# A diffusion trunk on one core: exchange loads on SyncE's queue, odd normalisation steps in x's tiles, first combinations ahead of the second split

## The chip, the core and the metric

The kernel runs on one core of a Trainium2 chip. TensorE (PE) multiplies, VectorE (DVE), ScalarE (ACT) and GpSimd (POOL) work on the elements, SyncE (SP) issues transfers, and ACT can issue them too, on a queue of its own. Each engine works through its own list in order; semaphores make one wait for another. The metric is the device time of one execution in microseconds: the median of three runs.

## The reference

One layer of a backbone with a context prefix, in float32: x is 2048 x 1024, the context 256 x 1024.

```
h  = rmsnorm(x) * (1 + sc1) + sh1
p  = h @ w_in                              # 1024 x 3584
o  = concat(hgrn2(p), gmlp_gate(p))        # two gated scans; gelu(u) * (W_s LN(gelu(v)) + b)
x  = x + g1 * (o @ w_out)                  # 1024 x 1024
h2 = rmsnorm(x) * (1 + sc2) + sh2
a, g = split(h2 @ w_up)                    # 1024 x 5632
m  = a * gelu(conv3x3(g) + conv_b)
x  = x + g2 * (m @ w_down)                 # 2816 x 1024
out = rmsnorm(x)
```

## The kernel before

**Arithmetic.** Each float32 operand is split into a rounded high part and the rest, both `fp32r`: a cast on ACT (`S.copy`, line 140) makes the high part, a subtraction (line 141) on DVE or POOL the low one. A product of two split operands is three matmuls (hi·hi, hi·lo, lo·hi). The projections behind the scans also use Strassen's scheme in Winograd's form: of four quarter blocks of each operand seven combinations are made, and seven products take the place of eight.

**Stages.** After the input projection, the scans and the gate (to about 925 us) comes the output projection: eight units of 256 rows, seven products each, 56 in all, numbered m here. Each product is 12 matmuls of 128x512 (`products`, line 1304): for k = 0 to 3 hi·hi and hi·lo in turn, then the four lo·hi. So the low part of the right operand B[i] is needed from the second matmul on, and its second half (k = 2, 3) from the sixth. Then the FFN's up-projection runs over the two halves of the tokens: 22 units each (`g` feeds the convolution, `a` is multiplied by its GELU), 154 products per half, numbered n. Here the right operands B[0] to B[6] are the seven combinations of the normalised y of one half; they stay for a whole half and are exchanged at n of about 143 to 166. The down-projection follows.

**Left operands.** `Unit.prep(i)` (line 1248) makes the split `Ah`, `Al` of combination i of a unit, three products ahead (`LOOK`): a cast on ACT, a subtraction on GpSimd. It also makes the next combinations in place: a21 = a11 - a21 (line 1264), s2 = a22 - a21 (1266), a11 = s2 + a11 (1268), a12 = a12 - s2 (1270), on DVE for the output projection and for the units marked `light`, on GpSimd otherwise. The first unit's halves lie in `ahead[0]` and `ahead[1]` (tiles `first`), its s2 in `ahead[4]`, the first two split pairs in `pairs_a`. `LEAD` interleaves the first two units: (0,0), (0,1), (0,2), (1,0), (0,4), (1,1), (0,3) and so on. Products 0 and 2 of a unit add into the same bank `ux`, which line 1407 reads and adds to the row tile after each product.

**Right operands.** B[i][1] is loaded raw; `in_place(i)` (line 924) casts it to B[i][0] on ACT (one instruction, line 927, always pinned) and subtracts in two halves on DVE (line 930). `apart(i, m)` puts the cast behind product m and the two halves behind product m+1. In the output projection B[1] is split during the last layer norm of the gate (line 716), B[2] beside the mixing that follows it (line 724).

**Normalisations.** `second_norm` (line 1317) works on one unit's rows behind its last product: the scaling (1326), then four steps k, each with four transposes into a bank `dn`, two ACT instructions (1341) into a tile of seven combinations, three DVE subtractions (1344 to 1346) and a store to `yd` (1347). A step's tile is `yf` for odd k of units 1 to 5, and otherwise `fl`, of which there are two buffers (`c_tile`). `fl` also holds s2 of every second FFN unit. `first` and `step` tell, in microseconds of a planner that counts TensorE's work, when the first step and the next ones may be put in; what is left at the end of the last unit is put in there (line 1431). `v_tile` has three buffers (`cv`): they hold rows of x and later the values of the convolution.

**The convolution's end and the exchange.** A value tile is written by GELU (line 1492), multiplied in place by the `a` products (1564, 1567) and stored by `put_m` (1530 and 1531). Near the end of half 0 the last GELU needs the buffer of the third last one. The raw B[j] of half 1 is issued on ACT's queue (line 1642) one product behind B[j]'s last use in half 0.

**Order.** A list planner orders each engine's instructions by its own estimates. `pin` puts an instruction behind the one traced before it on its engine; instructions without it can move ahead. SP issues the loads and stores in the order so planned and stands at each whose data or buffer isn't ready.

Of the kernel before, what the change touches and what calls it, by code (L numbers as in the profile page):

```python
# [9 lines left out]
F32 = mybir.dt.float32  # L10
# [8 lines left out]
P = 128  # L19
# [70 lines left out]
def tile_trunk(ctx, tc, x, c, cx, c_ctx, w_ada, b_ada, norm_mix, norm_ffn, w_in, hg_norm, sgu_g, sgu_b,  # L90
# [107 lines left out]
    with es1:  # L198
# [480 lines left out]
        def sgu(hh, h):  # L679

            z, u = {}, {}

            def both(n0):
                if n0 in z and n0 in u:
                    zt = z.pop(n0)
                    last = (hh, h) == (1, NH - 1)
                    (V if last else G).tensor_mul(zt, zt, u.pop(n0))
                    (S.dma_start if last and n0 else st)(oT_d[hh][:, 4 + h, n0:n0 + 512], zt)

            def su(n0, n, pj):  # L690
                u[n0] = pm.tile([P, 512], F32, tag="gu", name="gu", bufs=2)
                S.activation(u[n0], pj, AF.Gelu)
                both(n0)

            def sv(n0, n, pj):
                gv = pm.tile([P, 512], F32, tag="vv", name="gv", bufs=2)
                S.activation(gv, pj, AF.Gelu)

                def ln():
                    pt = bank("mi")  # L700
                    for i in range(4):
                        T.transpose(pt[:, i * P:(i + 1) * P], gv[:, i * P:(i + 1) * P], ident)
                    bs = pm.tile([P, 4, 6], F32, tag="bs", name="bs", bufs=2)
                    mv = pm.tile([P, 4, 2], F32, tag="mv", name="mv", bufs=2)
                    for i in range(4):
                        V.bn_stats(out=bs[:, i, :], in_=pt[:, i * P:(i + 1) * P])
                        V.bn_aggr(out=mv[:, i, :], in_=bs[:, i, :])
                    r = rstd(pm, mv[:, :, 1], 4, 1.0)
                    end = (hh, h) == (1, NH - 1)
                    nt = pm.tile([P, 512], F32, tag="nt", name="nt", bufs=2)  # L710
                    for i in range(4):
                        rooted.append(V.tensor_scalar(
                            out=nt[:, i * P:(i + 1) * P], in0=pt[:, i * P:(i + 1) * P], scalar1=mv[:, i, 0:1],
                            scalar2=r[:, i:i + 1], op0=ALU.subtract, op1=ALU.mult))
                    if end and n0:
                        in_place(1, pin)

                    def mix():
                        pz = bank("mi")
                        for i in range(4):  # L720
                            T.matmul(pz[:, i * P:(i + 1) * P], nt[:, i * P:(i + 1) * P], wsT[:, h, :],
                                     start=True, stop=True)
                        if end:
                            in_place(2, high=n0 == 0, low=n0 == 512)
                        V.scalar_tensor_tensor(out=nt.rearrange("p (c q) -> p c q", q=P),
                                               in0=pz.rearrange("p (c q) -> p c q", q=P), scalar=sgg[:, h:h + 1],
                                               in1=view(rh, h * P, [[0, 4], [1, P]]), op0=ALU.mult, op1=ALU.add)
                        z[n0] = nt
                        both(n0)
                    hg_q.later(mix, 7.0)  # L730
                hg_q.later(ln, 4.6)
            return su, sv

# [488 lines left out]
    def c_tile():  # L1222
        return px.tile([P, NK, P], F32R, tag="fl", name="fl", bufs=2)
# [4 lines left out]

    class Unit:
        def __init__(self, hh, kind, p, slots):  # L1230
            self.slots, self.light = slots, False
            self.hh, self.kind, self.f = hh, kind, 2 * p
            self.raw, self.A, self.s2, self.ready = [], {}, None, {}

# [13 lines left out]
        def prep(self, i):  # L1248

            a11, a21 = self.raw[0][:, :, :P], self.raw[0][:, :, P:]  # L1250
            a12, a22 = (self.raw[1][:, :, :P], self.raw[1][:, :, P:]) if i else (None, None)
            self.A[i] = self.ready.pop(i) if i in self.ready else a_tiles()
            hi, lo = self.A[i]

            if i == 1 and "s2" in self.ready:
                self.s2 = self.ready.pop("s2")
            elif i == 1:
                self.s2 = (c_tile()[:, :4, :].bitcast(F32) if self.slots[0] == 1 and self.kind != "o" else
                           px.tile([P, 4 * P + 80], F32, tag="s1", name="s2")[:, :4 * P].rearrange("p (k c) -> p k c", k=4))
            split(hi, lo, (a11, a12, self.s2, a11, a21, a12, a22)[i])  # L1260
            E = V if self.kind == "o" or self.light else G
            keep = pin if self.light or i == 1 else lambda i: i
            if i == 0:
                keep(E.tensor_sub(a21, a11, a21))
            elif i == 1:
                keep(E.tensor_sub(self.s2, a22, a21))
            elif i == 2:
                keep(E.tensor_add(a11, self.s2, a11))
            elif i == 3:
                keep(E.tensor_sub(a12, a12, self.s2))  # L1270
# [42 lines left out]
    with ExitStack() as esn, ExitStack() as esv:  # L1313
# [3 lines left out]
        def second_norm(n, xs, ss, bank_, first, step):  # L1317

            r = rstd(px, ss, 2, 1.0 / D)
            sc = []  # L1320
            t0 = T.t

            def scale():
                for i in range(2):
                    sc.append((pv[0] if n % 2 and n < NCH - 1 else px).tile([P, D], F32, tag="sc", name="sc", bufs=2))
                    scaled.append(pin(V.tensor_scalar(out=sc[i], in0=xs[i], scalar1=r[:, i:i + 1], scalar2=None,
                                                      op0=ALU.mult)))
            yield scale
            yield max(0.0, t0 + first - T.t)
            cl = slice(n % 4 * P, n % 4 * P + P)  # L1330
            for k in range(4):
                pt = bank_()
                for kk in range(2):
                    for i in range(2):
                        o = kk * 256 + i * P
                        T.transpose(pt[:, o:o + P], sc[i][:, (k + 4 * kk) * P:(k + 4 * kk + 1) * P], ident)
                fl = (pv[0].tile([P, NK, P], F32, tag="yf", name="yf", bufs=2) if k % 2 and 0 < n < NCH - 2 else
                      c_tile().bitcast(F32))
                for kk, dims in ((0, [[7 * P, 2], [1, P]]), (1, [[4 * P, 2], [1, P]])):
                    kq = k + 4 * kk  # L1340
                    pin(S.activation(view(fl, kk * P, dims),
                                     pt[:, kk * 256:kk * 256 + 256].rearrange("p (i c) -> p i c", c=P),
                                     AF.Identity, bias=s2[:, kq:kq + 1], scale=a2[:, kq:kq + 1]))
                pin(V.tensor_sub(fl[:, 3:5, :], view(fl, 7 * P, [[-2 * P, 2], [1, P]]), view(fl, 0, [[7 * P, 2], [1, P]])))
                V.tensor_sub(fl[:, 2, :], fl[:, 5, :], fl[:, 3, :])
                V.tensor_sub(fl[:, 6, :], fl[:, 1, :], fl[:, 2, :])
                st(yd[n // 4][:, :, k, cl], fl[:, :7, :])
                yield step

        pairs = [Unit(n // 4, "o", n % 4, (1, 2) if n % 2 else (3, 0)) for n in range(NCH)]  # L1350
        pairs[0].raw, pairs[0].ready = ahead[:2], {0: ahead[2], 1: ahead[3], "s2": ahead[4]}
        blocks = [(pairs[n], i) for n, i in LEAD] + [(u, i) for u in pairs[2:] for i in SEVEN]

        def prep_o(m):
# [6 lines left out]
            if i == 0 and n > 1:  # L1361
                (pairs + units)[n + 1].load()
            elif n == 1 and i == 2:
                pairs[2].load()
            elif n == NCH - 1 and i in (6, 5):
                units[1].load_half(6 - i)

        xts = {}

# [14 lines left out]
        with tc.issue_after(rooted[-1].ins), tc.issue_after(rooted[-5].ins):  # L1384
            for m in range(LOOK):
                prep_o(m)
        todo = {7: lambda: fetch_x(2, 0), 13: lambda: fetch_x(2, 1)}
        later, scales = {}, {}

        def apart(i, m):  # L1390
# [4 lines left out]
        for m, (u, i) in enumerate(blocks):  # L1395
# [28 lines left out]
                todo[m + 1] = lambda i=i: S.dma_start(B[i][1].bitcast(F32), yd[0][:, i])  # L1424
                apart(i, len(blocks) + (-3, -1, 0, 2, 3, 5, 7)[i])
            if i == 5:
                how = (9.0, 2.8) if n + 1 < NCH else (22.0, 5.5)
                norm = second_norm(n, xs, ss, lambda: dbank()[:, 0, :], *how)
                scales[m + (2 if n + 1 < NCH else 7)] = next(norm)
                if n == NCH - 1:  # L1430
# [186 lines left out]
    for n, (u, i) in enumerate(prods):  # L1617
# [20 lines left out]
            if n in t:  # L1638
                t.pop(n)()
        for j in range(7):  # L1640
            if last_use[j] == n - 1:
                S.dma_start(B[j][1].bitcast(F32), yd[1][:, j])
            elif 7 * NU - 14 + (6, 8, 10, 13, 15, 18, 20)[j] == n:
                apart(j, n)
        prep(n + LOOK)
        for g in later.pop(n, ()):
# [277 lines left out]
```

## Time and profile before

| | before |
|---|---|
| median of three runs | 2393.86 us (2393.09 to 2396.85) |
| the profiled execution | 2402.16 us |
| its span | 2400.4 us |
| mean granted TensorE clock | 0.988 |
| ACT busy | 1057.8 us (44%) |
| GpSimd busy | 945.0 us (39%) |

Lines of the timeline have start, duration, engine, line, operation, tiles and count, and in brackets the idle time in front of it and what ended that. `SPq` and `ACTq` are transfers at their issue; where several are merged, the duration runs from the first issue to the last. Lines of the waits have the engine, line and tile that waited, whom it waited for, total, times and the longest. In the windows, the first number after the stretch is its length, then come the busy times of the engines, the granted clock as a fraction, the mean share of the DMA engines and the rate.

### The profile page before, as it was taken

What the parts mean: (1) busy time and instruction counts of PE and PEld (TensorE: products, weight loads), DVE (VectorE), ACT (ScalarE), POOL (GpSimd) and SP (SyncE); (2) the same over time, 40 slices, a digit from 0 to 9 for tenths busy, and PEclk for the clock granted to TensorE, in tenths of its full rate; (3) what the DMA queues carried; (4) which work ended last, traced back from release to release, by engine and by line L of the source; (5) the groups of instructions that cost most, each with busy time, mean ns of one, the idle gap of its engine ahead of it and who ended that gap; (6) DMA issues with size and microseconds to landing.
All of it is one profiled execution on the core that took longest, in us unless ns stands there. A gap on an engine that the chain in (4) does not pass through costs nothing. (4 is left out here: it accounts for less than half of the span.)

```text
span 2400.4 us, 37036 instructions
## 1 busy us (share of the span) xinstructions
PE 2335.5 (97%) x14059; PEld 1925.5 (80%) x14059; DVE 1694.4 (71%) x2228; ACT 1057.8 (44%) x1811; POOL 945.0 (39%) x817
## 2 busy tenths in 40 slices
PE   7999999999999998998999999899999999999998
PEld 6887878878888876886888888688888888888887
DVE  3757786676686668777986666889677764776876
ACT  3554444443553544545544444354444443332343
POOL 0022111111122234544788787588787860000002
PEclk8999999999999999998999999999999999999999
DMA  8356445664444226766322223522223239834645
GB/s 300 122 187 191 159 145 184 208 228 149 162 159 141 80 93 224 237 229 234 106 82 92 76 91 96 195 75 97 91 84 101 77 126 395 263 123 157 226 148 202
DMA packets 285095, 379.95 MB, mean 158 GB/s; under 512 B 32213, under 2 KB 204525, under 8 KB 282229
## 3 DMA queue, kind: packets, MB, share of 16 engines
q1 hardware_dynamic: 279468, 361.88, 44.9%
q10 hardware_dynamic: 5449, 15.70, 2.0%
q8 instruction: 111, 1.82, 0.3%
q14 instruction: 67, 0.55, 0.1%
HBM read 276.79 MB, written 100.74 MB: 157 GB/s over the span
## 5 line engine op out<-in xcount | busy, mean ns | idle before, releaser
L1482 DVE SCALAR_TENSOR_TENSOR dn<-gp,taps,dn 128x1024 f32<-128x1024 f32 x352 | 450.3, 1286 | 105.5 <-ACT dn L1479 101.0
L141 POOL TENSOR_TENSOR Al<-raw,Ah 128x512 fp32r<-128x512 f32 x306 | 411.9, 1359 | 138.0 <-ACT Ah L140 75.4
L71 PE MATMUL dn<-thl,mhl 128*128 128x512 f32 x1680 | 381.0, 389 | 0.0
L71 PEld LDWEIGHTS dn<-thl,mhl 128*128 128x128 f32 x1680 | 315.3, 188 | 65.5 <-issue 0.2
L71 PE MATMUL pj<-xh,whi 128*128 128x512 f32 x896 | 367.0, 410 | 0.0
L71 PE MATMUL pj<-xl,whi 128*128 128x512 f32 x896 | 351.7, 393 | 0.0
L71 PE MATMUL pj<-xh,wlo 128*128 128x512 f32 x896 | 350.9, 392 | 0.0
L140 ACT CAST Ah<-raw 128x512 fp32r<-128x512 f32 x306 | 189.6, 620 | 256.7 <-PE ux L71 142.9
L71 PE MATMUL ux<-rest,Ah 128*128 128x512 f32 x832 | 208.2, 391 | 0.2
L71 PEld LDWEIGHTS pj<-xh,whi 128*128 128x128 f32 x896 | 168.7, 188 | 38.8 <-issue 7.2
L71 PEld LDWEIGHTS pj<-xh,wlo 128*128 128x128 f32 x896 | 168.5, 188 | 35.7
L71 PEld LDWEIGHTS pj<-xl,whi 128*128 128x128 f32 x896 | 169.0, 189 | 29.1
L71 PE MATMUL uz<-rest,Ah 128*128 128x512 f32 x624 | 186.3, 392 | 1.9 <-DVE rest L930 1.7
L71 PEld LDWEIGHTS ux<-rest,Ah 128*128 128x128 f32 x832 | 155.9, 188 | 33.1 <-issue 0.9
L592 POOL TENSOR_TENSOR K<-K,tot 128x512 f32<-128x512 f32 x40 | 64.2, 1605 | 251.1 <-DVE K L592 139.4
L71 PE MATMUL uz<-four,Ah 128*128 128x512 f32 x412 | 161.1, 391 | 0.5 <-ACT Ah L140 0.5
L141 DVE TENSOR_TENSOR wlo<-raw,whi 128x1024 fp32r<-128x1024 f32 x68 | 83.7, 1231 | 97.6 <-ACT whi L140 95.1
L1780 POOL TENSOR_SCALAR ra<-ss 128x1 f32<-128x1 f32 x8 | 3.9, 490 | 358.9 <-ACT jk L1771 358.9
L71 PEld LDWEIGHTS uz<-rest,Ah 128*128 128x128 f32 x624 | 117.2, 189 | 27.4 <-DVE rest L930 2.5
L140 ACT CAST whi<-raw 128x1024 fp32r<-128x1024 f32 x68 | 71.2, 1048 | 131.9 <-PE pj L71 100.0
L71 PE MATMUL ux<-wo,Ah 128*128 128x512 f32 x408 | 105.4, 400 | 13.4 <-DVE wo L930 7.2
L71 PE MATMUL ux<-four,Ah 128*128 128x512 f32 x416 | 106.5, 397 | 7.2 <-DVE x L1407 3.9
(366 smaller groups left out, 4416.5 us busy)
## 6 DMA issues: line engine op xcount, KB each, us to landing
raw<-in_w_up_dram SPq DMA_DIRECT2D x88, 512.0 KB, 3.6
mr<-m SPq DMA_DIRECT2D x85, 512.0 KB, 6.1
raw<-in_w_in_dram SPq DMA_DIRECT2D x68, 512.0 KB, 4.2
sT<-wd SPq DMA_DIRECT2D x88, 256.0 KB, 5.2
raw<-in_w_ada_dram SPq DMA_DIRECT2D x32, 512.0 KB, 4.0
m<-cv SPq DMA_DIRECT2D x22, 544.0 KB
raw<-in_w_down_dram SPq DMA_DIRECT2D x22, 512.0 KB, 3.7
wd<-raw SPq DMA_DIRECT2D x22, 512.0 KB, 3.7
```

The costliest lines, as they stand in the source:

```text
L71: return self.engine.matmul(out, lhsT, rhs, **kw)
L140: keep(S.copy(hi, raw))
L141: (eng or G).tensor_sub(lo, raw, hi.bitcast(F32))
L592: e.tensor_mul(view(K2, row * W + o, src), view(K, o, src), view(tot, t0, [[4, n], [ts, 2], [0, B]]))
L1482: V.scalar_tensor_tensor(out=cr, in0=gt[:, t // 3:t // 3 + RH, t % 3:t % 3 + GW], scalar=taps[:, t * NF + f:t * NF + f + 1], in1=cr, op0=A ...
L1780: G.tensor_scalar(out=a, in0=ss, scalar1=plus, scalar2=None, op0=ALU.add)
```

## The change

Three edits. **First combinations.** a21 and s2 of the first unit are made on DVE, pinned, in front of the split of B[1] in the gate's last layer norm; B[2]'s low halves and a11 are made behind product 0 of the output projection (`behind_first`), no longer beside the mixing; `prep` leaves out the three combinations so made (`done`); the first two units are `light`, so that their combinations are pinned; the gate's very last multiplication (line 687) moves from DVE to GpSimd, its store stays on ACT's queue. **Normalisation steps.** Steps 1 and 3 of the last unit and step 1 of the last but one take a `v_tile` in place of an `fl` tile; the steps of the last but one are 4.5 planned microseconds apart instead of 2.8. **Exchange.** The loads of B[0] to B[6] for half 1 go to SP's queue, issued three products behind the last use instead of one; the casts of B[1] to B[6] come one to three products later, the low halves with them.

```
-                    (V if last else G).tensor_mul(zt, zt, u.pop(n0))
+                    (V if last and not n0 else G).tensor_mul(zt, zt, u.pop(n0))
...
                     if end and n0:
+                        a, b, s2 = ahead[0], ahead[1], ahead[4]
+                        pin(V.tensor_sub(a[:, :, P:], a[:, :, :P], a[:, :, P:]))
+                        pin(V.tensor_sub(s2, b[:, :, P:], a[:, :, P:]))
                         in_place(1, pin)
...
-                            in_place(2, high=n0 == 0, low=n0 == 512)
+                            n0 or in_place(2, low=False)
...
-            self.slots, self.light = slots, False
+            self.slots, self.light, self.done = slots, False, ()
...
-            if i == 0:
+            if i in self.done:
+                pass
+            elif i == 0:
...
-                fl = (pv[0].tile([P, NK, P], F32, tag="yf", name="yf", bufs=2) if k % 2 and 0 < n < NCH - 2 else
-                      c_tile().bitcast(F32))
+                if k % 2 and 0 < n < NCH - 2:
+                    fl = pv[0].tile([P, NK, P], F32, tag="yf", name="yf", bufs=2)
+                elif n == NCH - 1 and k % 2 or n == NCH - 2 and k == 1:
+                    fl = v_tile()[:, :D].rearrange("p (k c) -> p k c", c=P)
+                else:
+                    fl = c_tile().bitcast(F32)
...
+        pairs[0].done = 0, 1, 2
+        pairs[0].light = pairs[1].light = True
...
+        def behind_first():
+            in_place(2, pin, high=False)
+            a11 = ahead[0][:, :, :P]
+            pin(V.tensor_add(a11, ahead[4], a11))
...
-        todo = {7: lambda: fetch_x(2, 0), 13: lambda: fetch_x(2, 1)}
+        todo = {0: behind_first, 7: lambda: fetch_x(2, 0), 13: lambda: fetch_x(2, 1)}
...
-                how = (9.0, 2.8) if n + 1 < NCH else (22.0, 5.5)
+                how = (9.0, 2.8 if n + 2 < NCH else 4.5) if n + 1 < NCH else (22.0, 5.5)
...
-            if last_use[j] == n - 1:
-                S.dma_start(B[j][1].bitcast(F32), yd[1][:, j])
-            elif 7 * NU - 14 + (6, 8, 10, 13, 15, 18, 20)[j] == n:
+            if last_use[j] == n - 3:
+                ld(B[j][1].bitcast(F32), yd[1][:, j])
+            elif 7 * NU - 14 + (6, 9, 12, 15, 18, 21, 23)[j] == n:
                 apart(j, n)
```

## The prediction

> **What bounds the kernel now.** I read the page's busy shares first, then the list of TensorE's waits over the whole span, then four windows, then the timeline of three of them.
>
> ```profile
> span 2400.4 us, 37036 instructions
> PE 2335.5 (97%) x14059; PEld 1925.5 (80%) x14059; DVE 1694.4 (71%) x2228; ACT 1057.8 (44%) x1811; POOL 945.0 (39%) x817
> ...
> PE ux L71 <- DVE wo L930: 7.2, 1, 7.2
> PE ux L71 <- ACT Ah L140: 6.2, 1, 6.2
> ...
> PE ux L71 <- DVE x L1407: 3.9, 1, 3.9
> ...
> PE ux L71 <- POOL Al L141: 2.9, 1, 2.9
> PE ux L71 <- DVE four L930: 2.4, 2, 2.3
> ```
>
> PE is busy 97% of the span, so only its holes can be won. Of the large single waits (columns: total, times, longest) all but those of the opening ada loads lie on `ux`, in three places, which are the places that the diff touches: the opening of the output projection, its hand-over to the FFN, and the exchange of y's two halves. The windows show what each costs, clock included (columns: length, PE busy, PEld, DVE, ACT, POOL, granted clock, DMA share, GB/s).
>
> ```profile
> 925.91:942.63 16.72, 12.87 (x52) 10.17 (x50) 16.58 (x17) 5.69 (x8) 9.04 (x6) 0.90 0.90 324
> 1102.68:1133.49 30.81, 19.78 (x65) 14.43 (x64) 22.16 (x23) 17.35 (x24) 14.31 (x9) 0.78 0.55 182
> 1536.05:1563.39 27.34, 18.27 (x62) 14.11 (x60) 15.82 (x14) 10.80 (x14) 14.84 (x10) 0.81 0.57 193
> 1170.00:1306.00 136.00, 136.00 (x602) 112.67 (x601) 107.03 (x102) 63.83 (x103) 107.65 (x94) 1.00 0.27 88
> ```
>
> The last row is undisturbed: 136.00/602 = 0.226 us a matmul, 2.71 us for a product of 12. The first window holds 4 products (10.8 us), so it loses 5.9; the second 5 products and four transposes (14.0), so it loses 16.8; the third 5 products (13.6), so it loses 13.8. These 36.5 us are all that this change can win. Part of each loss is the clock, granted at 0.78 to 0.90 there.
>
> **Part A, the opening of the output projection.**
>
> ```profile
> 923.85 2.53 POOL L141 TENSOR_TENSOR pairs_a<-first,pairs_a 128x512 fp32r<-128x512 f32 x2
> ...
> 925.20 3.40 DVE L930 TENSOR_TENSOR wo<-wo,four 128x1024 fp32r<-128x1024 f32 x2
> ...
> 928.52 2.35 DVE L930 TENSOR_TENSOR four<-four 128x1024 fp32r<-128x1024 f32 x2
> ...
> 932.05 0.68 DVE L687 TENSOR_TENSOR nt<-nt,gu 128x512 f32<-128x512 f32 x1
> 932.65 0.68 DVE L1266 TENSOR_TENSOR s<-first,first 128x512 f32<-128x512 f32 x1
> ...
> 933.36 0.62 ACT L140 CAST Ah<-s 128x512 fp32r<-128x512 f32 x1 [6.99 <-DVE s L1266]
> ...
> 935.48 2.83 PE L71 MATMUL ux<-four,Ah 128*128 128x512 f32 x8 [3.85 <-DVE x L1407]
> ...
> 936.95 3.94 DVE L930 TENSOR_TENSOR four<-four,rest 128x1024 fp32r<-128x1024 f32 x2
> ```
>
> DVE is the bound (16.58 of 16.72 busy). ACT waits 6.99 for s2, PE 3.85 for the add of product 0, both queued behind two splits. The change puts the subtractions of L1264 and L1266 (0.68 each) ahead of the first split, the second split's low halves (2.35) behind the add of product 0, and one multiplication of L687 (0.68) on GpSimd, in front of the Al of the next products there; its store stays on ACT's queue. Pinning the first two pairs' combinations adds no instruction.
>
> Worked out: the first DVE split took 3.40 where the second took 2.35, because POOL was busy to 926.4; the two subtractions meet the same 1.05, so they end near 927.7 and the first split near 930.1, 1.5 later than now (928.6). Product 1 starts at 925.91 + 2.71 = 928.6 and needs the second half only at its sixth matmul: it loses 0.5 to 1. L1407 then comes near 931.5, the second split's first half by 932.7 (by 2.35 for two) or 933.5 (by 3.94 for two, contended). So product 2 starts about 2.4 before 935.48, and its eight matmuls (2.83 for 8 x 0.226 = 1.81) win up to 1.0 of clock. Late next is DVE itself: the split of 936.95 must be done before product 4, and has only L687 and one deferred combination less in front, 1.4 us. I take -2.5, nearest to the shift of 2.4; bounds -4 (clock won too) and +1.5 (product 1 delayed, product 4 held by DVE).
>
> **Part B, the last two normalisations.**
>
> ```profile
> 1089.52 0.74 DVE L1326 TENSOR_SCALAR sc<-cv,rs 128x1024 f32<-128x1024 f32 x1
> ...
> 1095.29 0.51 SPq L1347 DMA_DIRECT2D yd<-fl  x1
> ...
> 1104.81 0.56 ACT L1341 ACTIVATE fl<-dn,s,a 128x256 f32<-128x256 f32 x1 [5.46 <-DMA yd<-fl]
> ...
> 1105.86 0.43 DVE L1344 TENSOR_TENSOR fl<-fl 128x256 f32<-128x256 f32 x1 [5.53 <-ACT fl L1341]
> ...
> 1109.01 2.35 DVE L930 TENSOR_TENSOR wo<-wo 128x1024 fp32r<-128x1024 f32 x2
> ...
> 1110.28 2.08 PE L71 MATMUL ux<-wo,Ah 128*128 128x512 f32 x4 [7.21 <-DVE wo L930]
> ...
> 1117.81 0.56 ACT L1341 ACTIVATE fl<-dn,s,a 128x256 f32<-128x256 f32 x1 [4.61 <-PE dn L75]
> ...
> 1119.20 0.68 DVE L1266 TENSOR_TENSOR fl<-raw 128x512 f32<-128x512 f32 x1
> ...
> 1125.45 2.08 PE L71 MATMUL ux<-four,Ah 128*128 128x512 f32 x4 [2.27 <-DVE four L930]
> ```
>
> This is one chain: step 2 of normalisation 6 wants the `fl` buffer of step 0, whose store went out at 1095.29 and released it only at 1104.81; ACT stands 5.46, DVE behind it 5.53, B0's low halves come at 1109.01, PE has stood 7.21. With step 1 in a tile of x's rows, step 2 takes the buffer of normalisation 5's last such step, stored long before; the wait of 5.46 goes. The tile taken is that of row block 6's second half, last read by the scaling at 1089.52. The wider steps (4.5 for 2.8 of the planner's microseconds) put step 1 one product later and step 2 behind the last product, so step 2's ACT and DVE work no longer stands before B0's low halves at all; it stands before B1's, in what is now ACT's idle time of 4.61. Normalisation 7 has no ACT wait on its stores: its tiles are worth nothing by themselves.
>
> B0's low halves come 5.5 earlier (1103.5) and with them PE's restart, 1104.8 for 1110.28. The later splits follow their casts and move along. Four matmuls after the stall took 2.08 for 0.90; with an idle of 1.7 instead of 7.21 some 1.5 of the clock returns. I take -7.0. Bounds: -12 if 2.27 and what follows it go too; 0 if the wait only moves: s2 of the second FFN unit (the L1266 at 1119.20) takes the `fl` buffer that step 2 stores from, and if DVE now reaches it eight microseconds sooner than 1119.20 it can stand there for that store, with B2's split queued behind it.
>
> Of the clock the rows show this: granted 0.78 over the second window, with a wait of 7.21 in it. The Trainium skill, "TensorE: Matmul & The Clock Gate", Part 1, says that the clock halves only after an idle window of about 3.4 us; by that rule the remaining idle of 1.7 would cost no clock, and Part B would give about -8.5, an estimate from that page; the slow matmuls behind the 2.27 at 1125.45 speak against a bound that sharp.
>
> **Part C, the exchange.**
>
> ```profile
> 1532.62 0.33 ACTq L1642 DMA_DIRECT2D four<-yd  x1
> 1534.07 0.34 SPq L1530 DMA_DIRECT2D m<-cv  x1
> ...
> 1543.45 0.97 ACT L1492 ACTIVATE cv<-dn 128x960 f32<-128x960 f32 x1 [11.93 <-DMA as<-cv]
> ...
> 1545.09 3.78 PE L71 MATMUL ux<-wo,Ah 128*128 128x512 f32 x8 [6.16 <-ACT Ah L140]
> ...
> 1558.28 2.08 PE L71 MATMUL ux<-wo,Al 128*128 128x512 f32 x4 [2.90 <-POOL Al L141]
> ...
> 1530.00:1535.00 5.00, 5.00 (x24) 4.14 (x23) 5.00 (x5) 1.52 (x2) 4.65 (x3) 1.00 0.94 321
> 1535.00:1540.00 5.00, 3.93 (x18) 2.92 (x16) 4.71 (x7) 0.00 (x0) 1.25 (x1) 1.00 0.95 297
> ...
> 1551.67 1.91 ACT L927 CAST rest<-rest 128x2048 fp32r<-128x2048 f32 x1
> ...
> 1568.83 1.98 PE L71 MATMUL ux<-four,Ah 128*128 128x512 f32 x8
> ...
> 1570.95 13.52 SPq L1241 DMA_DIRECT2D raw<-in_w_up_dram  x3
> ...
> SPq L1241 <- POOL Al L141: 38.2, 8, 14.5
> ```
>
> ACT's last GELU of half 0 waits for the buffer of an m tile whose store went out at 1534.07 and released it at 1543.45; queued behind it are the Ah of the first product of half 1, which PE waits 6.16 for, and two exchange loads on ACT's queue. Meanwhile the DMA engines are 0.94 to 0.95 busy: B4's 1 MB went out just ahead of that store.
>
> The change issues the loads from SP, two products later, and puts six of the seven splits one to three products later. Seven issues leave ACT (the row's 0.33 each, 2.3 us), worth nothing while it idles. If B4's load comes behind the store, the store is spared 1.05 MB at 0.297 to 0.321 MB/us, 3.4 us: GELU, Ah and PE move by 3.4. B2's cast now stands behind the Ah of the next products, which helps the wait of 2.90; against this, B4's to B6's low halves have two products (5.4 us) until they are needed, and took up to 3.94 with POOL beside them. I let these two cancel, and take -4.0 with 0.6 of clock. Bounds: -9 (both waits go) and +14, from the second rival.
>
> Sum: -2.5 - 7.0 - 4.0 = -13.5. The profiled execution took 2402.16 (its span and 1.8 around it) and would take 2388.7; it lies 8.3 over the median, so I take the difference from 2393.86: **2380.4 us**.
>
> **Rivals.** *The exchange gains nothing* (0.20): on one queue the transfers go out in issue order, so a load already ahead of the store keeps all of its megabyte in front, where two queues share the engines. Loads without a pin go when the buffer is free, and B3's, for one, is free before the store. For it speaks the 0.95 share; against it, that B4's last reader ends after the store's data are there. Part C is then 0: -9.5, 2384.4 us. The Trainium skill, "DMA: Bandwidth & Descriptors", Queues, rings and completion order, has the same: each engine takes turns between the queue rows by packet; its section Issuing engines are not separate DMA queues says that a second issuer saves only issue time. No run here shows it yet.
>
> *SyncE's queue blocks* (0.08, the slow side): SP stood 14.5 for a weight load's buffer, up to 1570.95. If B4 to B6 go out behind that wait, B4 lands some 8 us later (the store above took 9.4) and is split 4.3 after that (1.91 the cast, 2.35 the halves), near 1583; PE wants it two products behind 1568.83, at 1574.3. That is 9 us, 3 of clock as behind the 6.16, and 2 for B5: +14 against -9.5 from A and B, 2398.4 us. It decides if B4's load issues later than 1574.3 - 12.3, about 1562.
>
> *The waits only move* (0.15): DVE stands at that L1266, B2's split stays late, and DVE holds product 4 of Part A: B -2, A 0, C -1, together -3, 2390.9 us. For it speaks DVE's 16.58 of 16.72; against it, ACT's 4.61 of idle.
>
> **How the numbers follow.** The forecast has 0.52; 0.05 is left for more than that (all bounds near their good ends, -25, 2369). About 0.2%, 4.8 us, is what a measurement of this kernel tells from no change. Forecast, the first rival and the rest below are faster: 0.77; the third is within: 0.15; the second is slower: 0.08. The range runs from 2371 to 2393: it leaves out the second rival and the good ends, 0.13 together. The forecast's own range is 2374 to 2386.
>
> **What would show it.** A: PE's wait on L1407 near 935 gone or under 1, and the Ah of s2 some 5 us earlier. B: no ACT wait on yd's stores before 1110, PE's wait on B0's low halves under 2. C: ACT's wait at the last GELU of half 0 near 8 instead of 11.93, and no SP wait in front of an exchange load. It is wrong if PE's three windows still lose over 32 us together, or if a wait of PE on B3 to B6 appears in the exchange.

## The result and the profile after

| | before | after |
|---|---|---|
| median | 2394.23 us (8 runs, 2389.06 to 2401.44) | 2382.71 us (8 runs, 2378.45 to 2387.17) |
| ratio of after to before, 95% interval | | 0.995 [0.9936, 0.9965] |
| the profiled execution, its span | 2402.16, 2400.4 | 2383.78, 2382.0 |
| mean granted TensorE clock | 0.988 | 0.993 |

The change is faster by 12.0 us (8.4 to 15.3), for 13.5 forecast; this goes by the ratio, the medians differ by 11.5. Line numbers move in the changed kernel: the cast of `in_place` is L930 and its subtraction L933 (before 927 and 930), the add of each product L1423 (1407), the ACT step of the normalisation L1350 (1341), GELU L1508 (1492), the exchange load L1658 (1642), the stores of an m tile L1546 and L1547 (1530 and 1531).

First the page, then TensorE's waits over the whole span (total, times, longest), as for the kernel before.

```profile
span 2382.0 us, 37044 instructions
PE 2328.6 (98%) x14059; PEld 1915.9 (80%) x14059; DVE 1699.7 (71%) x2227; ACT 1057.7 (44%) x1811; POOL 947.7 (40%) x818
...
q10 hardware_dynamic: 4441, 8.36, 1.0%
```

```profile
PE ux L71 <- DVE four L933: 3.3, 1, 3.3
...
PE ux L71 <- DVE rest L933: 2.7, 4, 1.0
PE uz L71 <- DVE four L933: 2.4, 3, 1.0
...
PE ux L71 <- ACT Ah L140: 1.5, 1, 1.5
```

ACT's queue (q10) carries 8.36 MB where it carried 15.70: the seven exchange loads have left it. Of the four large waits of the kernel before (7.2, 6.2, 3.9, 2.9) none is left. In their place stand smaller ones, the longest 3.3, most of them on DVE's low halves (L933).

The windows show where (same columns as before). The first, third and fourth are the stretches of the prediction's three windows: from the first product of the output projection to the fifth, from the first product of the FFN to the sixth, and the five products at the exchange. The second follows on the first.

```profile
922.48:936.05 13.57, 11.86 (x52) 8.74 (x50) 13.54 (x12) 5.17 (x8) 7.81 (x6) 1.00 0.99 351
936.05:966.73 30.68, 26.00 (x98) 18.50 (x97) 23.39 (x23) 12.54 (x15) 18.13 (x12) 0.94 0.42 147
1101.09:1127.27 26.18, 19.55 (x70) 13.62 (x69) 21.08 (x21) 16.06 (x23) 13.59 (x9) 0.80 0.59 212
1529.86:1543.46 13.60, 13.60 (x62) 11.27 (x60) 13.60 (x11) 6.90 (x8) 11.34 (x8) 1.00 0.81 278
```

And the stretch of the kernel before that answers to the second row:

```profile
942.63:968.27 25.64, 23.95 (x97) 19.00 (x96) 17.66 (x18) 12.58 (x15) 14.07 (x11) 0.93 0.42 151
```

The five products at the exchange went from 27.34 to 13.60 and lose nothing more; the eight behind them lose 1.5, with one wait of 1.0. The opening's first four products went from 16.72 to 13.57, but the same products behind them take 30.68 for 25.64: the 3.15 won is given back with 1.9 on top. The first five products of the FFN take 4.6 less in this pair of executions.

Three stretches serve as measures below. *Opening*: the first product of the output projection to the first product of its last unit. *Hand-over*: from there to the sixth product of the FFN. *Exchange*: thirteen products from the start of the prediction's third window on (35.4 if none waits, at 2.72). Against the profiled execution of before the changed one has 158.44 - 155.92 = +2.52 in the opening, 46.35 - 51.66 = -5.31 in the hand-over, 36.91 - 49.10 = -12.19 in the exchange, and its first product of the output projection comes 3.43 earlier; together -18.41, the whole difference of the spans. Not all of that is the change: how much one execution differs from the next in each stretch, the experiments had to show.

### The profile page after: what moved, and what is told of

Read it like the earlier page. It is cut to its first block, busy times and chain, and to the rows that moved or that the text cites. A ratio compares the mean times of both kernels' runs of the same rounds, so it can differ in the third digit from the quotient of the medians.

```text
span 2382.0 us, 37044 instructions
## 1 busy us (share of the span) xinstructions
PE 2328.6 (98%) x14059; PEld 1915.9 (80%) x14059; DVE 1699.7 (71%) x2227; ACT 1057.7 (44%) x1811; POOL 947.7 (40%) x818
## 3 DMA queue, kind: packets, MB, share of 16 engines
q1 hardware_dynamic: 280476, 369.23, 46.2%
q10 hardware_dynamic: 4441, 8.36, 1.0%
## 4 chain that ended last, share of the span: by engine, by line
PE 50%; DVE 5%; issue 4%; DMA 1%; POOL 1%; ACT 1%; POOLq 0%; SPq 0%; DVEq 0%; ACTq 0%
PE ux L71 20%; PE uz L71 16%; PE dn L71 13%; DVE four L933 1%; DMA yd<-fl 1%; DVE rest L933 1%; DMA raw<-in_w_up_dram 1%; DVE odd L86 0%; PE dn L75 0%; POOL rr L1799 0%; POOL Al L141 0%; ACT mhl L140 0%; DVE raw L1275 0%; DVE sc L1331 0%; DVE wo L933 0%
## 5 line engine op out<-in xcount | busy, mean ns | idle before, releaser
L71 PE MATMUL uz<-rest,Al 128*128 128x512 f32 x416 | 112.2, 390 | 0.0
```

What stands on the lines that cost most here:

```text
L71: return self.engine.matmul(out, lhsT, rhs, **kw)
```

## The experiments

Ratios are to the kernel before on the same chip, with their 95% interval; gains in us are worked out from them. A ratio is not that of the two medians; the gains by the two differ by up to 3.7 us (pin_loads). The stretches are those of each run's one profiled execution.

| kernel | ratio | opening | hand-over | exchange |
|---|---|---|---|---|
| before | 1 | 155.92 | 51.66 | 49.10 |
| before_again | | 156.97 | 45.40 | 47.74 |
| only_A | 1.0004 [0.9994, 1.0014] | 157.26 | 47.54 | 49.55 |
| only_B | 0.9993 [0.9984, 1.0002] | 156.55 | 45.74 | 49.99 |
| only_C | 0.9959 [0.9947, 0.9971] | 155.87 | 47.21 | 36.54 |
| the change | 0.995 [0.9936, 0.9965] | 158.44 | 46.35 | 36.91 |
| gelu_first | 0.997 [0.9956, 0.9985] | 157.04 | 46.33 | 46.02 |
| pin_loads | 0.9934 [0.9908, 0.996] | 156.47 | 43.77 | 36.53 |
| C_ldonly | 0.995 [0.9934, 0.9966] | 155.81 | 50.33 | 36.69 |
| C_split | 0.9983 [0.9969, 0.9996] | 156.52 | 46.23 | 43.40 |
| BC_pin | 0.994 [0.9926, 0.9954] | 155.58 | 48.77 | 36.57 |
| B_tile | 0.9996 [0.9984, 1.0008] | 155.84 | 46.27 | 49.93 |
| A_nolight | 1.0002 [0.9992, 1.0012] | 156.62 | 46.75 | 47.35 |
| A_nopool | 1.0002 [0.9993, 1.0011] | 158.98 | 47.28 | 48.84 |

### Each part alone

Three kernels take one part of the change each, a fourth run is the kernel before once more. The edits are those of the diff above, divided as the prediction divides them.

> The kernel before with the first edit alone (first combinations ahead of the second split). Theory 1, read from the two traces: the gain at the opening is given back in the next ten products, because B3's, B6's and B5's splits are not moved by it; the time from the first product of the output projection to the last unit's first product was 155.9 before and 158.4 after, so 0 to +2.5 us, ratio 1.000 to 1.001. Theory 2, the prediction's term: -2.5 us, ratio 0.999.

> The kernel before with the second edit alone (the last two normalisations' odd steps in tiles of x's rows, steps 4.5 apart). Theory 1, from the traces: -5.3 us, ratio 0.998, ACT's wait on yd's store gone, PE's wait on B0's low halves under 1. Theory 2, the prediction's term: -7 us, ratio 0.997.

> The kernel before with the third edit alone (exchange loads on SP, later splits). Theory 1: the gain comes from ACT's order, in which the last GELU of half 0 now stands behind the Ah of four more products, not from the store's landing: PE loses nothing there any more, -9 to -13 us, ratio 0.9945 to 0.996, and the GELU still waits some 8 us behind its store's issue. Theory 2, the prediction's term: the store lands 3.4 us earlier and the time falls by 4 us, ratio 0.998.

> The kernel before, unchanged, for a second profile of it. Its first profile took 2402.16, some 8 us over the median. If the exchange's loss (13.8 us in the first profile) is the part that varies, it is smaller here; if the variation lies in untouched stages, the three windows lose 5.9, 16.8 and 13.8 again within 1 us.

Part C carries the gain: 9.8 us (7.0 to 12.7) of the change's 12.0. Part B is worth 1.7 (a loss of 0.5 to a gain of 3.8), Part A costs 1.0 (a gain of 1.4 to a loss of 3.4); neither can be told from nothing. The kernel before, profiled again, spans 2390.0 where the first profile had 2400.4; 6.3 of these 10.4 us lie in the hand-over, which took 45.40 for 51.66. Of the two cases in the expectation neither came as written: the three windows lose 5.6, 10.5 and 12.4 for 5.9, 16.8 and 13.8, so the exchange varies a little and the hand-over most. What the prediction took from the first profile as the price of that stage was one execution's.

### What moved the exchange

In the kernel before ACT's list has the last GELU of half 0 directly ahead of the Ah that PE waits 6.16 for. In the changed kernel it stands behind the Ah casts of that product and the next ones. ACT's timeline of the kernel before, around the GELU at 1543.45:

```profile
1530.90 0.62 ACT L140 CAST Ah<-raw 128x512 fp32r<-128x512 f32 x1
...
1544.32 0.21 ACT L1493 COPY edges<-dn 128x64 f32<-128x64 f32 x1
1544.41 0.63 ACT L140 CAST Ah<-raw 128x512 fp32r<-128x512 f32 x1
```

After:

```profile
1526.49 0.62 ACT L140 CAST Ah<-raw 128x512 fp32r<-128x512 f32 x1 [2.02 <-PE uz L71]
1529.19 0.62 ACT L140 CAST Ah<-raw 128x512 fp32r<-128x512 f32 x1 [2.09 <-PE uz L71]
1529.72 1.91 ACT L930 CAST four<-four 128x2048 fp32r<-128x2048 f32 x1
1531.91 0.62 ACT L140 CAST Ah<-raw 128x512 fp32r<-128x512 f32 x1 [0.28 <-issue]
1535.89 0.97 ACT L1508 ACTIVATE cv<-dn 128x960 f32<-128x960 f32 x1 [3.35 <-DMA as<-cv]
```

The GELU still waits for its store, but the Ah of three coming products and B2's cast are done by then, and no product waits for what is behind it. So one theory is the order of ACT's list; the rival, the prediction's, is the store that lands earlier because the loads no longer go in front of it.

**gelu_first** puts GELU back directly ahead of that Ah and leaves the rest:

```
-            split(hi, lo, (a11, a12, self.s2, a11, a21, a12, a22)[i])
+            split(hi, lo, (a11, a12, self.s2, a11, a21, a12, a22)[i],
+                  keep=pin if self is units[NU] and i == 0 else lambda i: i)
```

> The changed kernel, with one thing put back: the Ah cast of the first product of half 1 (product 153 counted from the half's 152nd) is pinned on ACT, so that the last GELU of half 0 stands directly ahead of it again. The loads stay on SyncE's queue, the splits stay late. Theory (the order of ACT's list made the gain of the exchange): PE's wait on that Ah comes back with some 5 us (the store lands near 8.5 us after its issue, GELU 0.97 and the cast 0.62 behind it, product 153 is due 5 us after the issue), products 152 to 157 take 22 to 27 us instead of 13.60, and the kernel takes 9 to 13 us more than the change, near 2392 to 2396. Rival (the loads' queue made it: the store lands early enough): the wait stays under 1.5 us, the five products stay under 16, and the time stays within 2 us of 2382.7.

ACT's timeline of gelu_first and the product behind it:

```profile
1532.18 0.97 ACT L1509 ACTIVATE cv<-dn 128x960 f32<-128x960 f32 x1 [10.98 <-DMA as<-cv]
...
1533.72 1.66 ACT L140 CAST Ah<-raw 128x512 fp32r<-128x512 f32 x3 [0.47 <-ACT edges L1510]
...
1534.40 3.58 PE L71 MATMUL ux<-wo,Ah 128*128 128x512 f32 x8 [4.42 <-ACT Ah L140]
```

The wait is back, 4.42 for the 5 expected. The five products take 19.8, under the 22 to 27 expected but far over the rival's 16, and the whole exchange takes 46.02, 9.1 more than in the change. The median is 2389.11 (2386.8 to 2391.5), 6.4 more than the change's on another chip, less than the 9 to 13 expected; by the ratios it is 4.8, and their intervals overlap. So the time by itself does not quite tell the two kernels apart; the wait and the stretch do, and their sign and place are those of the order theory. By its ratio gelu_first still gains 7.2 us, of which the exchange accounts for 1.3 to 4.0 (47.35 to 49.99 in the seven executions with the old exchange); where the rest lies these runs do not show. The loads were on SyncE's queue all the while, so the queue by itself did not make the gain.

**C_ldonly** and **C_split** divide Part C: the first only moves the loads to SP, with the old place and the old splits, the second only has the later splits.

```
-                S.dma_start(B[j][1].bitcast(F32), yd[1][:, j])
+                ld(B[j][1].bitcast(F32), yd[1][:, j])
```

```
-            elif 7 * NU - 14 + (6, 8, 10, 13, 15, 18, 20)[j] == n:
+            elif 7 * NU - 14 + (6, 9, 12, 15, 18, 21, 23)[j] == n:
```

> The kernel before with only the queue of the exchange loads changed: SyncE's in place of ACT's, at the old place in the program (one product behind the last use) and with the old splits. Order theory: with the loads' issues gone from ACT's list the planner puts the GELU behind the next products' Ah casts, so nearly the whole gain of the exchange is there: five products in 13.6 to 16 us, the kernel 8 to 10 us below the kernel before. Rival (the later casts and low halves made it): the PE wait on Ah goes but a wait of 3 to 6 us on a B operand's low halves takes its place, and the gain is under 5 us.

> The kernel before with only the later splits of the exchange; the loads stay on ACT's queue, one product behind the last use. Order theory: GELU still stands ahead of the first product's Ah, PE still waits some 6 us there, the second wait (2.9) may go: 0 to 4 us below the kernel before. Rival (B2's cast behind the Ah casts made it): both waits go, the five products take under 16 us, and the kernel gains 8 to 10 us.

C_ldonly has the whole gain, that of Part C and, by its ratio, that of the whole change: exchange 36.69, 12.0 us (8.1 to 15.8) below the kernel before. Its one PE wait there is 1.0, on ACT, none on low halves: the later issue and the later splits add nothing that these runs can tell.

C_split did not behave as either theory had it. It gains 4.1 us (1.0 to 7.4) by its ratio and 1.5 by the medians; the exchange is 4 to 6.6 shorter in the profiles. ACT's timeline shows why:

```profile
1526.36 0.62 ACT L140 CAST Ah<-raw 128x512 fp32r<-128x512 f32 x1
...
1538.00 0.97 ACT L1492 ACTIVATE cv<-dn 128x960 f32<-128x960 f32 x1 [11.02 <-DMA as<-cv]
...
1538.96 0.63 ACT L140 CAST Ah<-raw 128x512 fp32r<-128x512 f32 x1
```

```profile
1533.70 1.97 PE L71 MATMUL ux<-wo,Ah 128*128 128x512 f32 x8
1536.43 1.20 PE L71 MATMUL ux<-wo,Al 128*128 128x512 f32 x4 [0.75 <-POOL Al L141]
1539.64 2.14 PE L71 MATMUL uz<-rest,Ah 128*128 128x512 f32 x8 [2.02 <-ACT Ah L140]
```

GELU waits as long as ever (11.02), but one more Ah is ahead of it: the first product starts without a wait, and the second waits 2.02 in place of the first's 6.16. My expectation had GELU still ahead of the first Ah. With the loads still on ACT's queue, one cast's place ahead of a waiting instruction goes with an exchange shorter by some 4 us or more; that fits the order theory, from a side I had not foreseen.

**pin_loads** is the changed kernel with the exchange loads pinned on SP, which puts B3's and B4's behind the store.

```
-                ld(B[j][1].bitcast(F32), yd[1][:, j])
+                pin(ld(B[j][1].bitcast(F32), yd[1][:, j]))
```

> The changed kernel with the exchange loads pinned on SyncE's queue, so that B3's and B4's loads are issued behind the store of the second half of the m tile that GELU waits for, not ahead of it. It tests whether a load issued ahead of that store costs the store its time. The prediction's step (a store spared 1.05 MB lands 3.4 us earlier): the store lands 5 us or less after its issue for the 8.6 of the change, and ACT's wait at the GELU (3.35 in the change) is gone. Rival (what else is in flight sets the landing): 8 to 10 us still. For the time the order theory expects no change beyond 2 us, since no matmul waits for that GELU any more, unless B3's split, 3 us later, makes PE wait; then 2 to 5 us more with a PE wait on DVE's low halves near product 158 to 160.

SP's issues of the change, then of pin_loads, the latter with GELU:

```profile
1522.54 0.46 SPq L1658 DMA_DIRECT2D rest<-yd  x1
...
1526.42 0.32 SPq L1658 DMA_DIRECT2D four<-yd  x1
1527.27 0.32 SPq L1546 DMA_DIRECT2D m<-cv  x1
1527.64 0.42 SPq L1547 DMA_DIRECT2D as<-cv  x1
```

```profile
1524.45 0.32 SPq L1546 DMA_DIRECT2D m<-cv  x1
1524.82 0.42 SPq L1547 DMA_DIRECT2D as<-cv  x1
1525.34 0.65 SPq L1658 DMA_DIRECT2D rest<-yd  x1
...
1527.78 0.46 SPq L1658 DMA_DIRECT2D four<-yd  x1
...
1530.07 0.97 ACT L1508 ACTIVATE cv<-dn 128x960 f32<-128x960 f32 x1
```

In the change both loads (B3's is the row of 1522.54) go out ahead of the store (B4's at 1526.42, the store at 1527.27), and GELU gets its buffer 8.6 us after the store's issue; before it was 9.4. With the loads behind, GELU follows the cast in front of it without a wait, at most 5.6 after the issue. From the store's issue to GELU it is 7.6 to 8.7 us in the four executions with B4's load ahead on SyncE's queue (the change, only_C, C_ldonly, gelu_first) and at most 5.6 in the two with B3's and B4's behind (pin_loads, BC_pin). So the loads ahead of the store do cost it at least 2 to 3 us, near the prediction's 3.4; the change doesn't remove that. And it is worth nothing once no product waits for GELU: the exchange takes 36.53 for 36.91, the median is 2382.48 for 2382.71.

### The hand-over

**B_tile** has the tiles of the odd steps without the wider spacing.

> The kernel before with the tiles of the odd normalisation steps alone; the steps of the last but one unit stay 2.8 planned microseconds apart. Theory (the stall of 5.46 on a store was one execution's; the same code waited 0.5 to 1.0 there in four other runs): no ACT wait on a store of yd, the wait of PE on B0's low halves 0 to 2.5, the hand-over (last unit's first product to the sixth FFN product) 44 to 47 us, and a time within 2 us of the kernel before. Rival (the prediction's Part B): 5 us or more below the kernel before.

It is worth 1.0 us (a loss of 1.9 to a gain of 3.8), with no ACT wait on a store. All executions together say why. ACT's wait on the store of step 0 was 5.5 in the first profile of before and 0.5, 0.9, 1.0, 0.9, 1.0 and 1.4 in six of the seven others with the old tiles; in the seventh, C_ldonly, ACT stood 3.5 at the same instruction, which its trace puts down to PE. The hand-over took 47.8 in the mean of the eight (45.4 to 51.7). In the five with the whole of Part B it took 46.2 (43.8 to 48.8). In all five another wait has come up on ACT, 2.8 to 3.1 in four of them and 6.3 in BC_pin. The timeline of the change, SP and ACT first:

```profile
1094.41 0.52 SPq L1356 DMA_DIRECT2D yd<-fl  x1
1095.02 1.25 SPq L1244 DMA_DIRECT2D raw<-in_w_up_dram  x1
...
1099.76 0.62 ACT L140 CAST Ah<-raw 128x512 fp32r<-128x512 f32 x1 [2.94 <-DMA raw<-in_w_up_dram]
...
1100.38 3.43 DVE L933 TENSOR_TENSOR wo<-wo 128x1024 fp32r<-128x1024 f32 x2
...
1114.97 1.76 DVE L1275 TENSOR_TENSOR raw<-raw,s 128x512 f32<-128x512 f32 x1
...
1116.65 4.51 DVE L933 TENSOR_TENSOR four<-four 128x1024 fp32r<-128x1024 f32 x2
...
1119.00 2.07 PE L71 MATMUL ux<-four,Ah 128*128 128x512 f32 x4 [3.33 <-DVE four L933]
```

A weight load of the FFN, issued behind the store of step 0, now ends the wait; before, it landed while ACT stood for that store. B0's halves are earlier (in the change PE waits 0.6 for them at most), but B2's, the rows of `four<-four`, are hardly earlier than in most executions with the old tiles: in front of them DVE still makes the combinations of the second FFN unit, and GpSimd is at work beside their split, as in the kernel before:

```profile
1123.11 4.51 DVE L930 TENSOR_TENSOR four<-four 128x1024 fp32r<-128x1024 f32 x2
```

Counted from the FFN's first product, this split starts at 14.0 to 16.2 us in six executions with the old tiles (18.9 and 20.4 in the two in which ACT stood long) and at 14.3 to 18.2 in the five with Part B. PE waits 2.3 for it in each of the first eight and 2.3 to 5.3 in the five, 3.33 in the change.

### The opening

**A_nolight** is Part A without the pinning of the first two pairs' combinations, **A_nopool** Part A without the move of the last multiplication to GpSimd.

```
-        pairs[0].light = pairs[1].light = True
```

```
-                    (V if last and not n0 else G).tensor_mul(zt, zt, u.pop(n0))
+                    (V if last else G).tensor_mul(zt, zt, u.pop(n0))
```

> The first part alone, without the pinning of the first two pairs' combinations. Theory one (the pins make the cost: ACT's casts of B3 and B4 stand behind a pinned Ah that waits 4.50 for PE, and the low halves come one product late): the four PE waits on those low halves shrink from 2.7 to about 2 or less, and the stretch from P0 to the last unit's first product is 155 to 156.3 us for 157.26. Theory two (DVE is the bound there, and the pieces only change places): the stretch stays at 156.8 to 158.5.

> The first part alone, without the move of the last multiplication to GpSimd: DVE makes it. Theory one (the store of that product is issued by ACT, which stands 6.81 us for GpSimd with the Ah of s2 behind it): ACT's wait there is under 4, the Ah of s2 comes 2 us or more earlier, product 2 starts without its wait of 1.54, and the stretch from P0 to the last unit's first product is 155 to 156.3 us for 157.26. Theory two (DVE is the bound): 0.7 more of DVE ahead of the second split, PE waits on DVE for product 1 or 2 instead, and the stretch is 157 to 158.5.

A_nopool speaks against theory one: ACT's wait in front of s2's Ah falls from 6.81 to 5.91 only, product 2 starts 6.56 after product 0 for 7.47, and then stands on DVE instead, so that product 3 starts 12.62 after product 0 for 10.82. The opening takes 158.98, no better and a little over theory two's range. That fits theory two: DVE is the bound, and the pieces only change places. A_nolight is undecided: 156.62 lies between the two expectations, the waits on B3's and B4's low halves are 4.2 in three in place of 2.7 in four, and the time is that of the kernel before. All told, the opening took 155.58 to 156.97 in the eight executions without Part A (156.1 in the mean) and 156.47 to 158.44 in the four with all of it (157.3).

### Without Part A

**BC_pin** takes Parts B and C and the pin of the loads.

> The changed kernel without its first part (the opening of the output projection is that of the kernel before) and with the exchange loads pinned on SyncE's queue. If the first part costs time, as its run alone suggested (P0, the first product of the output projection, to the last unit's first product: 157.26 us for 156.27 in the mean of six runs without it), this takes 1 to 3 us less than the change: 2380 to 2382, with that stretch back at 155.8 to 157.0 and the wait of 3.8 on the add of product 0 back too. Rival (the first part gains its 2.5 as predicted): 2385, slower than the change. The pin is worth within 1 us.

Its median, on another chip, is 2380.92, the ratio 0.994 [0.9926, 0.9954], that of the change 0.995 [0.9936, 0.9965]: below both kernels by its median, but it can't be told from the change. The opening is back at 155.58, with the wait of 3.9 on the add of product 0. That Part A gains 2.5, by which BC_pin would be slower than the change, has nothing for it; that Part A costs something is likely and not shown.

## Why the prediction came out right, and which steps didn't

The time, the sign and the range held, but the sum was right through errors that cancel: -2.5, -7.0 and -4.0 were forecast, +1.0, -1.7 and -9.8 were measured part by part (together -10.5; the whole change measured -12.0). That the sum came near the forecast is luck.

**Part A: the start was right, what is late next was taken too low.** The two subtractions ended at 924.2, 1.7 after product 0 (forecast 1.8), product 2 started 7.48 after product 0 in place of 9.57, 2.1 earlier (forecast 2.4), and the wait on L1407 is gone. But s2's Ah came 6.81 after product 0 for 7.45, not 5 us earlier: the store of the multiplication moved to GpSimd is issued by ACT, and that Ah is behind it in ACT's list. The prediction named the store's queue and didn't ask who waits behind it. The step that failed is "late next is DVE itself": it put DVE 1.4 us better off in front of the split for product 4. DVE's timeline of the change, product 0 at 922.48:

```profile
921.76 1.72 DVE L717 TENSOR_TENSOR first<-first 128x512 f32<-128x512 f32 x1
923.52 0.69 DVE L718 TENSOR_TENSOR s<-first,first 128x512 f32<-128x512 f32 x1
...
927.06 0.68 DVE L1423 TENSOR_TENSOR x<-ux,x 128x512 f32<-128x512 f32 x1
927.66 3.40 DVE L933 TENSOR_TENSOR four<-four 128x1024 fp32r<-128x1024 f32 x2
930.99 1.79 DVE L1382 TENSOR_TENSOR first<-s,first 128x512 f32<-128x512 f32 x1
932.71 1.79 DVE L1269 TENSOR_TENSOR raw<-raw 128x512 f32<-128x512 f32 x1
```

Before, GpSimd stood idle from 0.5 to 8.2 us after product 0 (926.4 to 934.06), while DVE made its splits and combinations. Now it has the multiplication from 5.1 after product 0 on and the Al subtractions from 7.5 on, and DVE's work meets them: the moved split takes 3.40 for 2.35, the combination of L1382 1.79 for 0.69, that of L1269 1.79 for 1.19, 2.8 us together. The split for product 4 then starts 12.5 after product 0, where it was 11.0; the prediction had 9.6. That term was mis-sized by 2.9 us, and with it went the gain. The Trainium skill, "SBUF — State Buffer", Who interferes with whom, says that a VectorE operation with two SBUF inputs and a GpSimd operation that reads SBUF take turns whole, and the second waits until the first is done. The trace agrees in the rows above: GpSimd was at work to 922.94, from 927.57 to 928.85 and from 929.98 on, and the rows that begin in those stretches are the slow ones.

**Part B: the stall was real, its price was one execution's.** No ACT wait on a store of yd and a wait on B0's low halves under 2 were forecast, and both hold in the change; in BC_pin, with the same Part B, PE stood 3.5 for those halves, behind the weight load. The mis-sized term is the 5.5 us by which B0's halves come earlier: ACT's wait that was to go was 0.5 to 1.4 in six of the seven other executions with the old tiles, and the rival *The waits only move* describes the rest, with B2's split held up on DVE. DVE does not stand for a store there, as the rival had it, but is busy with the combinations; and the wait that came up first, a weight load on ACT, wasn't on the list. The -2 of that rival is near the measured -1.7, whose interval includes no gain. The remark on the clock was sound in its doubt. The Trainium skill, "TensorE: Matmul & The Clock Gate", Part 1, has the clock fall after an idle window of about 3.4 us; here a shorter one was enough: in all seven executions with Part C's old loads and splits an idle of only 2.90 or 2.91 was followed by a granted clock of 0.5, and sixteen matmuls then took 5.1 to 6.5 for 3.6.

**Part C: the mechanism was wrong, the place was right.** The step that failed is "If B4's load comes behind the store, the store is spared 1.05 MB": it stays ahead, as the rival *The exchange gains nothing* said, and the store takes 8.6 for 9.4. By the prediction's reasoning Part C should then have been near 0. It was -9.8, its good bound (-9, "both waits go"), by a way that the text touched in half a sentence (B2's cast behind the next Ah): it read from the trace of before that the Ah is queued behind GELU, and took ACT's order as given. The order is the planner's, and moving the loads off ACT's list alone (C_ldonly) moved GELU behind the next casts; why the planner does so was not tested. The seven issues that left ACT were costed at nothing because ACT idles; their cost was not their 2.3 us but where the list put the instruction behind them. ACT's wait at GELU is 3.35 (forecast 8), for the same reason. The Trainium skill, "DMA: Bandwidth & Descriptors", Issuing engines are not separate DMA queues, says that another issuer saves only issue time; for the transfers that is what the store's 8.6 and 9.4 show, and the time came from the issuer's list.

**SyncE's queue** did not block: B4's load went out at 1526.42, long before the 1562 from which it would have decided. Two of the prediction's signs failed all the same. SyncE did stand in front of exchange loads, 2.5 us for B0's and 1.7 for B4's, until PE had read the buffer for the last time; and PE did wait on one of B3 to B6, 1.03 us for B4's low halves. All that PE lost behind the five products is 1.5 us. The three windows lose 2.7, 12.2 and nothing, together 14.9 (limit 32), at a cost of 5 behind the first.

## What to carry to other kernels

Where an engine works in order, look at what stands behind each instruction that waits for a far transfer, and ask what the edit does to that order before asking what it does to the transfer: one GELU behind three casts instead of ahead of them was worth 10 us, a store landing 3 us earlier nothing. A stall at a buffer that a store gives back differs from execution to execution (0.5 to 5.5 us here), so take a second profile of the same kernel before it goes into a sum. Work moved forward on a bound engine is priced with what its new neighbours do, not with its old row.

## What was unexpected of the hardware

What a stall costs afterwards depends on where it falls, not on its length alone. In the kernel before, the second wait of 2.90 was followed by four matmuls in 2.08; in before_again one of 2.91 by four in 1.20:

```profile
1547.56 1.20 PE L71 MATMUL ux<-wo,Al 128*128 128x512 f32 x4 [2.91 <-POOL Al L141]
...
1549.11 0.63 PE L71 MATMUL uz<-four,Ah 128*128 128x512 f32 x1
1549.53 0.63 PE L71 MATMUL uz<-wo,Ah 128*128 128x512 f32 x1
```

There it is the next product whose matmuls come slowly, 0.43 us apart. The granted clock (the 0.50 and 1.00 in the windows) shows the same slow stretch in both, only placed otherwise, first the kernel before, then before_again:

```profile
1554.38:1557.79 3.41, 1.00 (x5) 0.49 (x3) 3.41 (x3) 0.00 (x0) 3.41 (x2) 1.00 0.28 114
1557.79:1561.20 3.41, 2.92 (x7) 2.35 (x8) 3.20 (x2) 0.75 (x2) 3.41 (x3) 0.50 0.08 30
```

```profile
1545.57:1548.98 3.41, 1.42 (x6) 1.20 (x7) 3.41 (x3) 0.13 (x1) 3.41 (x2) 1.00 0.35 144
1548.98:1552.39 3.41, 3.41 (x10) 2.67 (x9) 1.30 (x1) 3.29 (x4) 3.41 (x3) 0.50 0.69 238
```

Half clock begins 0.5 us before PE starts again in the one and 1.4 behind it in the other, and sixteen matmuls behind the wait take 5.11 and 5.37 us for 3.6: nearly the same price. In the traces of all fourteen executions the stretches of half clock, but for those cut off by the end of the span, are 3.41 us long or two or three times that, and their edges within a trace lie whole multiples of 3.41 us apart. Of the seven executions with this wait, five have one such stretch behind it and two (only_B, B_tile) have two, where the sixteen matmuls take 6.53. In those two PE started again 0.9 us after the stretch began, in the five 0.3 to 0.5 after or 1.3 to 1.4 before it.

A wait of 2.02 left the clock at 1.0 and eight matmuls at 2.14 for 1.98 (C_split), one of 4.42 left them at 3.58 (gelu_first).
